# Layer 0's late modulation rows: 32 row products issued inside the attention instead of behind it

## The chip, the core and the metric

The kernel runs on one core of a Trainium2 chip. The metric is the device time of one execution in microseconds (us); less is better. TensorE (PE) multiplies matrices, with its weight loads listed apart (PEld); VectorE (DVE) and ScalarE (ACT) do elementwise work and reductions, GpSimd (POOL) some subtractions, and the queue of SyncE (SP) issues every DMA of this kernel.

## The reference, cut to what matters

Two layers run over 1024 latent tokens and 128 context tokens, 1152 columns in all, of width 1024. Each layer has six modulation vectors for each of the two groups:

```python
def ada_modulation(cond, w_ada, b_ada):
    m = jax.nn.silu(cond) @ w_ada + b_ada
    return jnp.split(m[:, None, :], N_ADA, axis=-1)   # sh1, sc1, g1, sh2, sc2, g2
...
xs = xs + g1_s * ms
xs = xs + g2_s * channel_mixer(modulate(xs, norm_mlp[i], sh2_s, sc2_s), mlp1[i], mlp2[i])
```

Layer 0's `ms` comes from a pooling mixer and an attention of 8 heads. The parts sh2, sc2 and g2 are not needed before layer 0's MLP.

## The kernel before, in words

The activations lie transposed, features on partitions. Precise products are three matmuls of split operands (`mm3`: high by low, low by high, high by high, L335 to L337).

**Modulation rows.** Parts sh1 and sc1 of layer 0 are computed by matmuls. The other parts come from `ada_gen`: 128 modulation values are one tile `f` of 128 weight rows by 1024 (`wada`, 512 KB, two buffers), and for each of the two conditions one DVE instruction multiplies the tile by `silu` (the condition, spread over all partitions) and sums each row (L200, with a read of the accumulator behind it). I call it a row product. When eight tiles are done, `ada_bias` adds the bias (L210, and L214 for the scales). Layer 0's tiles 16 to 31 run as background work in the input projection; the 16 tiles 32 to 47 (sh2, sc2, g2: 32 row products) are the late ones. `bg` is a list of generators, and `background()` takes one step, that is one row product.

**Layer 0's attention.** `max_units` of head h+2 runs beside `attend_units` of head h: 24 score matmuls (`ps_m`, L1034) whose row maxima the DVE takes (L1035); `ps_m` has three PSUM banks, so the fourth matmul waits for the first reduction. The maxima go through `put_max` (L1016, L1020, DMAs to `mrow` and into row 96 of `qh`). `attend_units` has two halves of nine key tiles: three score matmuls (L1070, L1073, L1074), an exponential on ACT, and the value matmul (`ps_pv`, L1077); `finish_values` copies the sum out on the DVE (L1001). For every second head `recip_pair` divides (ACT, POOL L1045, DVE L1046 and L1047).

**Behind the attention.** `x` is loaded again, the pooled and attention outputs are split (`split_groups`, L874 and L875), and `out_group` multiplies them by the output weights, two groups of 384 matmuls (`ps_o`), each tile added to `x` on the DVE (L889). The output weights are split by ACT and, for the low part, POOL (L161). Behind group 0 stand the statistics of the MLP's norm (L271 and L272 on DVE and POOL, then a matmul `ps_n`, L274) and the MLP's operands (L252 to L257, L311, L353). The MLP's first matmul is L422.

The order on each engine is set by a scheduler, by what is ready and by the order of the program, so an instruction may run far from its line. SBUF beyond the constants is 36 slots; the slot longest free is taken next.

Of the kernel before, what the change touches and what calls it, by code (L numbers as in the profile page):

```python
# [35 lines left out]
NEARLY = 2  # L36
# [54 lines left out]
def hybrid_kernel(ctx: ExitStack, tc: tile.TileContext, I, O):  # L91
# [8 lines left out]
    S = Slots(spool, NSLOT)  # L100
# [5 lines left out]
    def PS(name, tag="pa"):  # L106
        return psum.tile([P, 512], F32, tag=tag, name=name, bufs={"pa": 3, "pb": 3, "pc": 2}[tag])
# [4 lines left out]
    def dma(out, in_):  # L112
        nc.sync.dma_start(out.bitcast(F32) if out.dtype == F32R else out,
                          in_.bitcast(F32) if in_.dtype == F32R else in_)

    def run(g):
        for _ in g:
            pass

    def chain(*gs):  # L120
        for g in gs:
            yield from g
# [3 lines left out]
    def after(i, j):  # L126
        tc.add_manual_dep(i.ins, j.ins.name, NOSYNC, reason="order")
        return i
# [24 lines left out]
    def W(tag, name=None):  # L153
        return wpool.tile([P, 1024], F32 if tag == "wr" else F32R, tag=tag, name=name or tag, bufs=3 if tag == "wr" else 4)
# [25 lines left out]
    silu = []  # L180

    def silu_load():
        silu[:] = [S.alloc(f"silu{i}") for i in range(2)]
        for i in range(2):
            dma(silu[i][:, :D].rearrange("p (k f) -> p k f", k=KD), silu_d[:, i, :].partition_broadcast(P))

    def free_silu():
        S.free(*silu)
        yield
# [3 lines left out]
    def ada_gen(layer, fs, ring=False):  # L193
        rs = [] if ring else [S.alloc("wada") for _ in range(2)]
        for f in fs:
            r = W("wr", "wada") if ring else rs[f % 2]
            dma(r[:, :D], I["wada1"][f] if layer else I["wada0t"][f - 16])
            for i in range(2):
                a = ada[layer][:, f, i:i + 1]
                nc.vector.tensor_tensor_reduce(trash, r[:, :D], silu[i][:, :D], scale=1.0, scalar=0.0,  # L200
                                               op0=ALU.mult, op1=ALU.add, accum_out=a)
                yield
            if f % 8 == 7:
                ada_bias(layer, f // 8, ada[layer][:, f - 7:f + 1, :])
        S.free(*rs)

    def ada_bias(layer, part, src):
        a = ada[layer][:, 8 * part:8 * part + 8, :]
        b0 = VEC[f"bada{layer}"][0] + 8 * part
        nc.vector.tensor_add(a, src, vec[:, b0:b0 + 8].unsqueeze(2).to_broadcast([P, 8, 2]))  # L210
        if part in (1, 4):
            n0 = VEC[("nmix" if part == 1 else "nmlp") + str(layer)][0]
            nb = vec[:, n0:n0 + 8].unsqueeze(2).to_broadcast([P, 8, 2])
            nc.vector.scalar_tensor_tensor(a, a, 1.0, nb, op0=ALU.add, op1=ALU.mult)  # L214
# [21 lines left out]
    bg = []  # L236

    def background(n=1):
        for _ in range(n):
            while bg:  # L240
                try:
                    next(bg[0])
                    break
                except StopIteration:
                    bg.pop(0)
# [733 lines left out]
    def load_rest(h):  # L979
        ql, kl, v = S.alloc("ql", F32R), S.alloc("kl", F32R), S.alloc("v")  # L980
        n0, r0 = 64 * (h % 2), 32 * (h % 4)
        dma(ql[0:64, :NS], qd_n[1][h // 2, n0:n0 + 64, :])
        dma(ql[64:96, :NS], qd_r[1][h // 4, r0:r0 + 32, :])
        dma(kl[0:64, :], kd_n[1][h // 2, n0:n0 + 64, :])
        dma(kl[64:96, :], kd_r[1][h // 4, r0:r0 + 32, :])
        load_pv(vd0, h, v)
        return ql, kl, v
# [7 lines left out]
    def load_pv(vd, h, v):  # L995
        o = 192 * (h // 2) + 64 * (h % 2)
        dma(v.rearrange("p (t f) -> p t f", t=9), vd[:, :, o:o + P].rearrange("t p f -> p t f"))

    def finish_values(par, half, po, opair, den, last, store=None):
        qs = slice(half * 512, half * 512 + 512)  # L1000
        nc.vector.tensor_copy(opair[par:par + 64, qs], po[par:par + 64])  # L1001
        nc.scalar.copy(den[par:par + 64, qs], po[64 - par:128 - par])

        def divide():
            recip_pair(opair, den)
            if store is not None:
                dma(store, opair[:, :NS])
                S.free(opair)

        if last:  # L1010
            deferred.append(divide)
# [40 lines left out]
    def later(n=1):  # L1052
        for _ in range(n):
            if deferred:
                deferred.pop(0)()

    def attend_units(h, qk, rest, opair, den):
        (qh, kh), (ql, kl, vv) = qk, rest
        v = vv.rearrange("p (t f) -> p t f", t=9)
        held = None  # L1060
        for half in range(2):
            qs = slice(half * 512, half * 512 + 512)
            po = PS("ps_pv", "pc")
            for kt in range(9):
                if held is None:
                    held, n = S.alloc("p"), 0
                u = slice(512 * n, 512 * n + 512)
                ks = slice(kt * P, kt * P + P)
                ps = PS("ps_st")
                st = nc.tensor.matmul(ps, kl[0:96, ks], qh[0:96, qs], start=True, stop=False)  # L1070
                if len(mxi) >= LAG:
                    after(st, mxi[-LAG])
                nc.tensor.matmul(ps, kh[0:96, ks], ql[0:96, qs], start=False, stop=False)  # L1073
                nc.tensor.matmul(ps, kh[0:97, ks], qh[0:97, qs], start=False, stop=True)  # L1074
                p_ = held[:, u]
                nc.scalar.activation(p_, ps, AF.Exp, scale=scale0)
                nc.tensor.matmul(po, v[:, kt, :], p_, start=kt == 0, stop=kt == 8)  # L1077
                n += 1
                if n == 2:
                    S.free(held)  # L1080
                    held = None
                if kt == 6:
                    later()
                yield
            finish_values(64 * (h % 2), half, po, opair, den, half and h % 2)
        yield
# [4 lines left out]
    weave((chain(max_units(0, qks[0]), max_units(1, qks[1])), 50), (chain(value_gen(), context_gen0()), 17),  # L1091
          (mix_gen(), 13))
    rest = load_rest(0)
    opairs = []
    for h in range(8):
        if h % 2 == 0:
# [13 lines left out]
    S.free(oat)  # L1110


    def ada_late():
        silu_load()
        yield from ada_gen(0, range(16 + 8 * NEARLY, 48))
        S.free(*silu)

    x = [S.alloc(f"x{k}") for k in range(KD)]
    for k in range(KD):
        dma(x[k], I["xT"][k])  # L1120
    acts = [split_groups(o) for o in pooled]
    run(ada_late())
    acts += [split_groups(o) for o in opairs]
    out_group(0, 0, [a[0] for a in acts])
    for a in acts:
# [459 lines left out]
```

## Time and profile before

| | |
|---|---|
| three runs | 3025.92, 3026.92, 3040.58 us; median 3026.92 |
| profiled execution | 3023.98 us, its span 3022.2 us |
| granted TensorE clock, mean | 0.972 of full speed |
| busy | PE 96%, PE weight loads 86%, DVE 71%, ACT 44%, POOL 10% |
| late row products | between 564 and 637 us |
| attention, first score matmul to last value matmul | 312 to 563 us |
| first MLP matmul | 695 us |

The profile is of one execution. A busy PE row is not PE at its peak: consecutive matmuls overlap in the records, so the distance from start to start is what one costs. Idle time in front of an instruction carries the name of what ended it.

### The profile page before, as it was taken

The numbers are of one execution on the slowest core, as the hardware profiler recorded it, in microseconds if no ns is written. First come the engines' busy times: TensorE is split into PE (matmuls) and PEld (weight loads), VectorE is DVE, ScalarE is ACT, GpSimd is POOL, SyncE is SP. The second block draws the span as 40 slices with busy tenths as digits, with TensorE's granted clock in tenths as the row PEclk, the third lists the DMA queues.
The fourth block names the chain that finished last, engine by engine and source line by source line (L and its number), as shares of the span: only waits on it lengthen the run. The fifth ranks groups of instructions, "written<-read, shape, count | busy, mean of one in ns | idle before, by whom it ended". The sixth has DMA issues, their size and how long they took to land.

```text
span 3022.2 us, 46490 instructions
## 1 busy us (share of the span) xinstructions
PE 2910.4 (96%) x18302; PEld 2611.2 (86%) x18302; DVE 2160.5 (71%) x3921; ACT 1330.5 (44%) x2177; POOL 312.7 (10%) x210
## 2 busy tenths in 40 slices
PE   7998999889999999999999999998989999999999
PEld 4956666689999999999988888665889999999999
DVE  5977343797668889777789533677687678777765
ACT  5364344243436543453634522443244355453432
POOL 2004000143000020000221000000030000110000
PEclk9996999999999999999999999998999999999999
DMA  6529331432322334322556537796303232332322
GB/s 234 168 64 318 86 77 44 129 119 77 101 81 92 105 119 154 91 84 84 171 162 214 178 129 194 198 240 165 108 28 99 78 98 84 116 99 78 98 78 87
DMA packets 148268, 372.37 MB, mean 123 GB/s; under 512 B 14225, under 2 KB 67073, under 8 KB 148050
## 3 DMA queue, kind: packets, MB, share of 16 engines
q1 hardware_dynamic: 148050, 369.40, 40.0%
q8 instruction: 144, 2.36, 0.3%
q14 instruction: 74, 0.61, 0.1%
HBM read 310.69 MB, written 57.47 MB: 122 GB/s over the span
## 4 chain that ended last, share of the span: by engine, by line
PE 84%; DVE 6%; DMA 6%; issue 2%; ACT 1%; POOL 1%; SPq 0%; DVEq 0%; POOLq 0%; ACTq 0%
PE ps L452 9%; PE ps L454 9%; PE ps L453 9%; PE ps L422 8%; PE ps L424 8%; PE ps L423 8%; PE ps_pv L1077 4%; PE ps_n L335 2%; PE ps_n L336 2%; PE ps_n L337 2%; DVE trash L200 1%; PE ps_pv L1330 1%; PE ps_v L1354 1%; PE ps_v L1356 1%; PE ps_v L1355 1%
## 5 line engine op out<-in xcount | busy, mean ns | idle before, releaser
L452 PE MATMUL ps<-ml,wh 128*128 128x288 f32 x2048 | 591.9, 295 | 10.3 <-DVE ml L441 7.8
L453 PE MATMUL ps<-mh,wl 128*128 128x288 f32 x2048 | 600.8, 295 | 0.0
L454 PE MATMUL ps<-mh,wh 128*128 128x288 f32 x2048 | 596.6, 295 | 0.0
L422 PE MATMUL ps<-bl,wh 128*128 128x288 f32 x1792 | 532.9, 298 | 13.4 <-DVE bl L353 10.2
L423 PE MATMUL ps<-bh,wl 128*128 128x288 f32 x1792 | 529.7, 296 | 0.0
L424 PE MATMUL ps<-bh,wh 128*128 128x288 f32 x1792 | 528.2, 295 | 0.0
L452 PEld LDWEIGHTS ps<-ml,wh 128*128 128x128 f32 x2048 | 381.2, 188 | 11.3 <-DVE ml L441 8.3
L453 PEld LDWEIGHTS ps<-mh,wl 128*128 128x128 f32 x2048 | 385.1, 188 | 0.0
L454 PEld LDWEIGHTS ps<-mh,wh 128*128 128x128 f32 x2048 | 383.2, 188 | 0.1
L458 DVE SCALAR_TENSOR_TENSOR x<-ps,ada,x 128x288 f32<-128x288 f32 (+2 forms) x640 | 270.1, 451 | 119.1 <-PE ps L454 117.6
L422 PEld LDWEIGHTS ps<-bl,wh 128*128 128x128 f32 x1792 | 336.9, 188 | 16.7 <-issue 11.5
L424 PEld LDWEIGHTS ps<-bh,wh 128*128 128x128 f32 x1792 | 338.4, 189 | 0.0
L423 PEld LDWEIGHTS ps<-bh,wl 128*128 128x128 f32 x1792 | 337.6, 188 | 0.2
L395 ACT CAST wh<-s 128x512 fp32r<-128x512 f32 x256 | 146.1, 618 | 307.0 <-PE ps L454 216.7
L160 ACT CAST wh<-wr 128x1024 fp32r<-128x1024 f32 x188 | 196.9, 1049 | 165.7 <-PE ps L424 79.9
L200 DVE CUSTOM_DVE_ANT_0 trash<-wada,silu 128x1024 bf16<-128x1024 f32 x160 | 217.1, 1357 | 18.2 <-DMA wada<-in_wada 7.6
L161 DVE TENSOR_TENSOR wl<-wr,wh 128x1024 fp32r<-128x1024 f32 x144 | 179.6, 1251 | 44.3 <-ACT wh L160 44.3
L395 ACT CAST wh<-wr 128x1024 fp32r<-128x1024 f32 (+1 forms) x128 | 107.0, 836 | 220.0 <-PE ps L454 155.5
L161 POOL TENSOR_TENSOR wl<-wr,wh 128x1024 fp32r<-128x1024 f32 x44 | 122.2, 2784 | 708.7 <-ACT wh L160 687.4
L1035 DVE TENSOR_REDUCE stat<-ps_m 128x1 f32<-128x384 f32 x192 | 98.3, 552 | 117.0 <-PE ps_m L1034 116.7
L396 DVE TENSOR_TENSOR wl<-s,wh 128x512 fp32r<-128x512 f32 x232 | 157.6, 711 | 5.1 <-ACT wh L395 2.8
L1279 DVE CUSTOM_DVE_ANT_0 trash<-ps_m,ta 128x512 bf16<-128x512 f32 (+1 forms) x128 | 83.5, 652 | 98.1 <-PE ps_m L1277 90.4
(315 smaller groups left out, 6113.8 us busy)
## 6 DMA issues: line engine op xcount, KB each, us to landing
wr<-in_w SPq DMA_DIRECT2D x256, 512.0 KB
wada<-in_wada SPq DMA_DIRECT2D x48, 512.0 KB
wada<-in_wada0t SPq DMA_DIRECT2D x32, 512.0 KB
wr<-in_win SPq DMA_DIRECT2D x24, 512.0 KB
wr<-in_wout SPq DMA_DIRECT2D x24, 512.0 KB
vd<-vst SPq DMA_DIRECT2D x27, 384.0 KB
kk<-kd SPq DMA_DIRECT2D x32, 288.0 KB
nv<-vd SPq DMA_DIRECT2D x16, 576.0 KB
```

Source lines behind the costliest of these rows:

```text
L160: nc.scalar.copy(hi, r)
L161: (nc.gpsimd if e else nc.vector).tensor_sub(lo, r, hi)
L200: nc.vector.tensor_tensor_reduce(trash, r[:, :D], silu[i][:, :D], scale=1.0, scalar=0.0, op0=ALU.mult, op1=ALU.add, accum_out=a)
L395: nc.scalar.copy(h, src)
L396: (nc.gpsimd if j in EDGE and min(ps) in EDGE_POOL else nc.vector).tensor_sub(l, src, h)
L422: nc.tensor.matmul(ps, wh[:, a], hl[:, b], start=k == 0, stop=False)
L423: nc.tensor.matmul(ps, wl[:, a], hh[:, b], start=False, stop=False)
L424: nc.tensor.matmul(ps, wh[:, a], hh[:, b], start=False, stop=k == 3)
L452: nc.tensor.matmul(ps, wh, hl, start=kk == 0, stop=False)
L453: nc.tensor.matmul(ps, wl, hh, start=False, stop=False)
L454: nc.tensor.matmul(ps, wh, hh, start=False, stop=kk == 3)
L458: nc.vector.scalar_tensor_tensor(x[m][:, a:b], ps[:, a - ch * HC:b - ch * HC], g, x[m][:, a:b], op0=ALU.mult, op1=ALU.add)
```

## The change

The 16 late tiles move into the attention. `silu` is loaded, and the generator that makes the products is put on the background list, ahead of the loop over heads; each half head takes two steps of it, at its key tiles 2 and 6, which makes 2 x 2 x 8 = 32. What is left in the list is drained where the late products stood.

```diff
@@ attend_units
                 if kt == 6:
                     later()
+                if kt in (2, 6):
+                    background()
                 yield
@@ ahead of the heads
     rest = load_rest(0)
+    silu_load()
+    bg.append(chain(ada_gen(0, range(16 + 8 * NEARLY, 48)), free_silu()))
@@ behind the heads
-    def ada_late():
-        silu_load()
-        yield from ada_gen(0, range(16 + 8 * NEARLY, 48))
-        S.free(*silu)
-
     acts = [split_groups(o) for o in pooled]
-    run(ada_late())
+    background(10 ** 6)
     acts += [split_groups(o) for o in opairs]
```

The scheduler moves them further. On the DVE, where head 2's maxima begin (just ahead of head 0's first score matmul), there stood before (`ctxw` is the context's softmax, `o` the output of a pair of heads):

```order
L1016 TENSOR_REDUCE stat<-stat 128x8
L1099 COPY o_315_2581<-oat_2166 128x128
L910 TENSOR_REDUCE ctxw_2454<-ps_s 128x4
L911 TENSOR_SCALAR ctxw_2454<-ctxw_2454 128x4
L1035 TENSOR_REDUCE stat<-ps_m 128x1 x7
L916 RECIPROCAL ctxw_2454<-ctxw_2454 128x4
L1035 TENSOR_REDUCE stat<-ps_m 128x1 x2
```

and there stands now:

```order
L910 TENSOR_REDUCE ctxw_2454<-ps_s 128x4
L200 ISA trash,ada_91<-wada_2638,silu_315_2581 128x1024
L200 ISA ada_91 128x1
L1035 TENSOR_REDUCE stat<-ps_m 128x1
L911 TENSOR_SCALAR ctxw_2454<-ctxw_2454 128x4
L1035 TENSOR_REDUCE stat<-ps_m 128x1
L200 ISA trash,ada_91<-wada_2638,silu_316_2582 128x1024
L200 ISA ada_91 128x1
L1035 TENSOR_REDUCE stat<-ps_m 128x1 x3
L916 RECIPROCAL ctxw_2454<-ctxw_2454 128x4
```

The third product stands ahead of head 2's first maximum and the fourth between its second and third; the first two stand just ahead of this piece. From head 0's first score matmul on, the products and maxima ahead of the first L1001 are 13 and 11, ahead of the second 8 and 5, ahead of the third 7 and 9: all 32 are through in the first half of head 1. In the same three half heads of before there are 11, 9 and 9 maxima.

Behind the attention the DVE had, from the last split of the attention's output (`oa`) to the third tile of `x`:

```order
L875 TENSOR_TENSOR oa_4297<-o_495_3910,oa_4297 128x576
L200 ISA trash,ada_91<-wada_4223,silu_573_4219 128x1024
L200 ISA ada_91 128x1
L889 SCALAR_TENSOR_TENSOR x_553_4179<-ps_o,ada_91,x_553_4179 128x288
L200 ISA trash,ada_91<-wada_4223,silu_574_4220 128x1024
L200 ISA ada_91 128x1
L889 SCALAR_TENSOR_TENSOR x_553_4179<-ps_o,ada_91,x_553_4179 128x288
L889 SCALAR_TENSOR_TENSOR x_554_4180<-ps_o,ada_91,x_554_4180 128x288 x2
L200 ISA trash,ada_91<-wada_4224,silu_573_4219 128x1024
```

and has now, from the division of the last pair of heads (L1046) on:

```order
L1046 SCALAR_TENSOR_TENSOR den_3955<-den_3955,ry_4229 128x1024
L1047 SCALAR_TENSOR_TENSOR o_499_3954<-o_499_3954,den_3955 128x1024
L874 CAST oa_4291<-o_438_3495 128x576
L874 CAST oa_4294<-o_499_3954 128x576
L874 CAST oa_4297<-o_499_3954 128x576
L875 TENSOR_TENSOR oa_4291<-o_438_3495,oa_4291 128x576
L875 TENSOR_TENSOR oa_4294<-o_499_3954,oa_4294 128x576
L875 TENSOR_TENSOR oa_4297<-o_499_3954,oa_4297 128x576
L889 SCALAR_TENSOR_TENSOR x_557_4235<-ps_o,ada_91,x_557_4235 128x288 x2
L889 SCALAR_TENSOR_TENSOR x_558_4236<-ps_o,ada_91,x_558_4236 128x288 x2
```

No product is left between them. On PE the order differs only here: the first `ps_n` stands behind 400 output matmuls instead of 411 and the MLP's first matmul behind 368 more instead of 357; from there on PE's order is that of before. 25 output matmuls stand ahead of the last value matmul instead of 28.

In the queue of SP the loads of the attention's start now have products' tiles among them; `kh`, `ql`, `kl` and `v` are head operands, and the last `wada` below waits until its buffer's two products are done:

```order
L113 DMA wada_2637<-in_wada0t 128x1024
L113 DMA vd_486<-vst_2404 128x768
L113 DMA ql_2588<-qdn_479 64x1024
L113 DMA qh_2173<-mrow_2171 1x1024
L113 DMA ql_2588<-qdr_481 32x1024
L113 DMA wada_2638<-in_wada0t 128x1024
L113 DMA wr<-in_wout 128x1024
L113 DMA kl_2589<-kdn_483 64x1152
L113 DMA kl_2589<-kdr_485 32x1152
L113 DMA v_2575<-vd_486 128x9x128
```

Before, `wr`, head 0's row `qh`, head 2's `qh` and `kh` and then `v` stood in this place, and head 2's `kh` stands now ahead of the first `wada`.

## Rows read from the trace of the kernel before

**Rows 1.** The waits of PE between 560 and 700 us: who waited for whom, in us in total, times, and the longest.

```profile
PE ps_o L335 <- DVE oa L875: 10.8, 1, 10.8
PE ps_n L274 <- DVE nt L272: 8.9, 1, 8.9
PE ps_o L335 <- DVE x L889: 4.0, 2, 3.2
```

**Rows 2.** Stretches of the span: from:to, length, then busy us and count of PE, PE's weight loads, DVE, ACT and POOL, the granted clock, the DMA share and GB/s. The first is head 0's two halves and the first half of head 1, the second the other attention, the third from the last value matmul to the first `ps_n`, the fourth from there to the MLP.

```profile
312.28:361.90 49.62, 49.62 (x176) 32.50 (x175) 16.08 (x33) 18.99 (x33) 0.00 (x0) 0.99 0.25 59
361.90:563.40 201.50, 201.50 (x710) 130.22 (x709) 83.61 (x150) 82.46 (x139) 7.12 (x3) 1.00 0.27 73
563.40:637.80 74.40, 54.02 (x386) 52.85 (x385) 70.11 (x98) 16.24 (x26) 26.98 (x13) 0.90 0.46 149
637.80:694.90 57.10, 53.88 (x360) 53.26 (x361) 50.35 (x68) 24.81 (x39) 29.27 (x11) 0.89 0.21 65
```

**Rows 3.** PE in order of time behind the attention: start, us, line, names, and in brackets the idle time ahead with its releaser.

```profile
574.17 0.29 PE L337 MATMUL ps_o<-oa,wh 128*128 128x288 f32 x1
585.22 0.61 PE L335 MATMUL ps_o<-oa,wh 128*128 128x288 f32 x1 [10.75 <-DVE oa L875]
585.62 0.44 PE L336 MATMUL ps_o<-oa,wl 128*128 128x288 f32 x1
585.86 0.44 PE L337 MATMUL ps_o<-oa,wh 128*128 128x288 f32 x1
...
637.78 1.33 PE L274 MATMUL ps_n<-nt,ones 128*128 128x288 f32 x2 [8.88 <-DVE nt L272]
...
686.00 0.61 PE L335 MATMUL ps_o<-oa,wh 128*128 128x288 f32 x1 [3.21 <-DVE x L889]
...
693.73 0.29 PE L337 MATMUL ps_o<-oa,wh 128*128 128x288 f32 x1
...
695.07 0.29 PE L422 MATMUL ps<-bl,wh 128*128 128x288 f32 x1
```

**Rows 4.** DVE and POOL in order of time behind the attention, same columns.

```profile
569.15 3.25 DVE L200 CUSTOM_DVE_ANT_0 trash<-wada,silu 128x1024 bf16<-128x1024 f32 x1 [0.80 <-DMA wada<-in_wada0t]
576.92 1.22 DVE L1046 SCALAR_TENSOR_TENSOR den<-den,ry 128x1024 f32<-128x1024 f32 x1
579.21 1.22 DVE L1047 SCALAR_TENSOR_TENSOR o<-o,den 128x1024 f32<-128x1024 f32 x1
581.86 0.82 DVE L874 CAST oa<-o 128x576 fp32r<-128x576 f32 x2
584.41 1.42 DVE L875 TENSOR_TENSOR oa<-o,oa 128x576 fp32r<-128x576 f32 x2
640.60 1.92 DVE L210 TENSOR_TENSOR ada<-ada,vec 128x16 f32<-128x16 f32 x1
643.24 0.44 DVE L252 TENSOR_SCALAR nt<-ps_n 128x288 f32<-128x288 f32 x1
...
568.92 2.39 POOL L1045 TENSOR_TENSOR den<-den,ry 128x1024 f32<-128x1024 f32 x1 [56.13 <-ACT ry L1044]
571.52 3.13 POOL L161 TENSOR_TENSOR wl<-wr,wh 128x1024 fp32r<-128x1024 f32 x1 [0.20 <-ACT wh L160]
```

**Rows 5.** The row products by line: first the DVE's busy time in those between 563 and 640 us (two records each), then two neighbours of the early products, a stretch of these in which POOL rests, and the DVE's idle time ahead of the products of all 64 products of layer 0.

```profile
563.00:640.00 77.00, 52.67 (x64) 0.89 0.45 146
...
82.74 1.22 DVE L200 CUSTOM_DVE_ANT_0 trash<-wada,silu 128x1024 bf16<-128x1024 f32 x1
84.01 1.23 DVE L200 CUSTOM_DVE_ANT_0 trash<-wada,silu 128x1024 bf16<-128x1024 f32 x1
...
80.00:100.00 20.00, 20.00 (x117) 20.00 (x116) 18.78 (x38) 5.67 (x13) 0.00 (x0) 1.00 0.50 158
...
  DMA wada<-in_wada0t: 7.0, 10
```

**Rows 6.** The attention's first half heads in order of time: score matmuls for the maxima and the value matmul that follows them on PE, three maxima, and the copies that end the first and the third half head.

```profile
318.41 0.69 PE L1034 MATMUL ps_m<-kh,qh 96*128 96x384 f32 x3
318.93 1.02 PE L1077 MATMUL ps_pv<-p,v 128*128 128x512 f32 x2
...
314.43 1.49 DVE L1035 TENSOR_REDUCE stat<-ps_m 128x1 f32<-128x384 f32 x3 [2.25 <-PE ps_m L1034]
...
330.36 0.68 DVE L1001 COPY o<-ps_pv 64x512 f32<-64x512 f32 x1
361.91 0.69 DVE L1001 COPY o<-ps_pv 64x512 f32<-64x512 f32 x1
```

**Rows 7.** Head 2's first maxima, ahead of the attention: the issue of its `kh` on SP, PE's and the DVE's first instruction on it, and the stretch 305 to 310 us with the columns of Rows 2.

```profile
295.53 0.45 SPq L113 DMA_DIRECT2D kh<-kdn  x1
...
303.72 0.76 PE L1034 MATMUL ps_m<-kh,qh 96*128 96x384 f32 x3 [2.48 <-DMA kh<-kdr]
...
304.17 3.34 DVE L1035 TENSOR_REDUCE stat<-ps_m 128x1 f32<-128x384 f32 x7 [2.64 <-PE ps_m L1034]
...
305.00:310.00 5.00, 4.93 (x14) 2.88 (x13) 5.00 (x13) 0.00 (x0) 0.23 (x1) 0.61 1.15 256
```

**Rows 8.** One late tile: its issue on SP and the product that waited for it.

```profile
629.08 0.33 SPq L113 DMA_DIRECT2D wada<-in_wada0t  x1
...
632.83 1.23 DVE L200 CUSTOM_DVE_ANT_0 trash<-wada,silu 128x1024 bf16<-128x1024 f32 x1 [0.15 <-DMA wada<-in_wada0t]
```

## The prediction

> **What bounds the kernel now.** I began with PE's waits by releaser, since PE is the engine that is nearly always busy. Around the moved products three stand out, all of them on the DVE: 10.8, 8.9 and 4.0 us [rows 1]. PE's order of time says where. PE stops after 574.17 + 0.29 us and starts again at 585.22, when the DVE has split the last pair of heads (L875); it stops again ahead of the first `ps_n` at 637.78, for L272, and at 686.00 for an L889. Behind the first stop the output matmuls follow each other by 585.86 - 585.62 = 0.24 us, where undisturbed they need (695.07 - 693.73) / 10 = 0.134 us, the first of those rows and the last being ten matmuls apart [rows 3]. The distance is nearly twice as long: TensorE was at its lower level, 1.2 instead of 2.4 GHz, after standing still for 10.75 us. The stretches say why the DVE is late. From 563.4 to 637.8 it is busy 70.11 of 74.40 us [rows 2], and 52.67 us of this are the late row products [rows 5].
>
> The attention is the opposite. From 312.28 to 361.90 the DVE is busy 16.08 of 49.62 us, from there to 563.40 it is busy 83.61 of 201.50 [rows 2]. PE never rests there.
>
> **What the change gives back behind the attention.** From the last value matmul to the MLP's first matmul the kernel takes 74.40 + 57.10 = 131.5 us [rows 2]. The order leaves 743 output matmuls there; at 0.134 us [rows 3] they need 99.6 us. So 31.9 us are waits, low level and the `ps_n` matmuls. What will remain of them:
> - The division of the last pair still ends it. POOL's L1045 ends at 568.92 + 2.39 = 571.3; behind it the DVE has L1046 and L1047 (1.22 each), three L874 (0.41) and three L875 (0.71) [rows 4], together 5.8 us, to 577.1. PE has work until 574.5 + 3 x 0.134 = 574.9, as three more output matmuls are left behind the last value matmul. A stop of 2.2 us, and up to 2 at the low level behind it; I take 1.
> - The `ps_n` matmuls and their wait. The first `ps_n` has 40 output matmuls between itself and the tile it depends on, 5.4 us, for an addition to `x`, a square, two sums. I take 1 us for the wait (0 to 3) and 2 for the matmuls, two of which are in the row of 1.33 us [rows 3].
> - The stop of 3.21 us for L889 [rows 3]. Today L252 starts at 643.24, 4.1 us after its `ps_n` can be done (637.78 + 1.33), with products' leftovers, L210 of 1.92 us among them, ahead of it [rows 4]. That lateness goes, so I take half, 1.6 us (0 to 3.2).
>
> About 7 us remain (4 to 13): 24.5 us come back (19 to 28).
>
> **What the products cost in the attention.** A product takes 84.01 - 82.74 = 1.27 us from start to start where POOL rests [rows 5]. The late ones take 52.67 / 32 = 1.65 us on average, since one that runs beside POOL's L1045 or L161 takes 3.25 us [rows 4, 5]. The Trainium skill (SBUF — State Buffer, Who interferes with whom) says that a DVE instruction with two SBUF inputs and a GpSimd instruction that reads SBUF exclude each other; the trace agrees here, 3.25 us beside POOL and 1.22 without. By that rule the moved products would take 1.27 us, as POOL rests in these half heads; by today's mean, 28 of them would take 28 x 0.38 = 10.6 us more. I take 1.27 us, since POOL is busy 0.00 us in the first stretch [rows 2].
>
> *Ahead of head 0.* Here the DVE sets the pace: 5.00 of 5.00 us busy from 305 to 310 us [rows 7]. Of the four products there, two lie in idle time (2.64 us, while the load of head 2's `kh` is awaited). The third waits for the second `wada`, which stands behind more loads, and holds up the first maximum; the fourth costs 1.27 us, while two maxima (0.50 each [rows 6]) move behind the start. That makes 0.3 us if the tile is there, and 6 if the third comes some 5 us late. I take 3.
>
> *The first three half heads.* The DVE has to do, from head 0's first score matmul: 28 products, 35.6 us; 25 maxima at 0.50, 12.5; two L210 at 1.92; three L1001 at 0.68 [rows 4 to 6]; 0.5 of small things: 54.4 us. PE needs 49.6 us today, and with four score matmuls fewer (0.52 for three [rows 6]) 48.9. The excess is 5.5 us. It is worst in the first half, 24.6 us of DVE work against 330.36 - 312.28 = 18.1 of PE's, or 6.4 us. It reaches PE because the DVE works in order: a late product holds up the maxima, these the three banks of `ps_m`, and these PE, which has the score matmul in the middle of its own order. If the banks take up the excess, 2 us remain. I take 5.5 (2 to 6.4).
>
> *Late tiles.* Fourteen of the sixteen loads can start only when the two products on their buffer are done, and SP waits there with head 3's loads and the next rows of maxima behind it; these are needed half a head later and more. The DVE waited 7.0 us for tiles of layer 0 over 64 products [rows 5]; half of it, 3.5 us, for 32 (0 to 7). In today's late place nothing hangs on such a wait that the products don't already hold up; in the attention the maxima do.
>
> *POOL* splits two output weights around head 0's start; one may meet a product: 0 to 2.1 us, I take 0. ACT and its exponentials are not touched, and the extra 9 MB of loads lie in stretches with a DMA share of 0.25 to 0.27 [rows 2].
>
> Together 3 + 5.5 + 3.5 = 12 us (2.3 to 21.5).
>
> **Sum.** 24.5 - 12 = 12.5 us less than the profiled 3023.98: 3011.5. The median of the runs is 2.94 us above the profiled execution, which makes 3014.4, say **3014 us**, 0.4% below 3026.92. The ends are 28 - 2.3 = 25.7 us faster and 19 - 21.5, 2.5 us slower.
>
> **The rivals.**
> - *The attention swallows the products.* The DVE has 33.5 us idle in the first stretch and 118 in the second [rows 2]. If the lag runs on behind the banks until the products are through, only the start (about 3 us) is paid: 24.5 - 3 = 21.5 less, **3005 us**. Against it: the order packs 28 products, 35.6 us, into those 33.5.
> - *The tiles land late.* Head 2's `kh` took 303.72 - 295.53 = 8.2 us from its issue to PE's start on it [rows 7]; a late tile took 632.83 - 629.08 = 3.75 [rows 8]. With 8.2 us throughout, two buffers give four products per 2 x 1.27 + 8.2 + 0.3 = 11 us; seven such rounds make 77 us from about 304, so to 381 instead of 361.9. With the start that is 22 us: **3024 us**, no change. For it speaks the crowded queue at the start, against it the share of 0.25 behind that.
> - *Something else binds behind the attention.* Without a product in it the DVE is busy 50.35 of 57.10 us in the fourth stretch, and POOL 29.27 [rows 2]. If only half of the 24.5 us comes back, **3027 us**.
> - *TensorE falls to its lower level in the paced half heads*: the rival on the other side. Where maxima paced PE from 305 to 310 us the granted clock was 0.61 [rows 7]. At the lower level the 48.9 us of PE's work take 0.24 / 0.134 times as long, 38.7 us more: 3014.4 + 38.7 = **3053 us**. It uses up the forecast's 12.5 us once 16 us of PE's work run so. Against it: only one in four or five of PE's matmuls there waits for a maximum, while from 305 to 310 nearly each one did. [...]
>
> **How the numbers follow.** The forecast has 40 in 100, with 3012 to 3021 as its own range; the swallowed products 32, late tiles 14, a second bound behind the attention 6, the lower level 8. The predicted time is that of the forecast. 3003 to 3027 leaves out the lower level and the tails of the others. Half a per cent, 15.1 us, is about what a measurement can tell from no change. Faster by more than that: the swallowed products and the forecast's better end, 0.37; within it 0.55; slower, the lower level, 0.08.
>
> **What would show it.** Right: no product behind 563 us; PE's stop ahead of L875 2 to 3 us long, that of L272 under 3; some 105 to 110 us from the last value matmul to the MLP's first; head 0's first score matmul some 3 us later than at 312.3, and the third L1001 some 12 us later than at 361.9, with PE waiting for L1035. Wrong: third L1001 within 4 us of before (swallowed) or 20 later (late tiles, with waits of the products for `wada`); a granted clock below 0.9 in these half heads; a long stop behind the attention that names POOL or ACT.

## The result, and the profile after

The changed kernel takes 3012.06 us (median of 7 runs, 3006.6 to 3018.45) against 3026.92 (seven runs of before beside it). The ratio is 0.994, with a 95% interval of 0.9926 to 0.9954: 0.5 to 0.7% faster. In two more comparisons it came to 0.9942 and 0.9955. The forecast was 3014. One run of the experiments below (products_in_heads_6_7, 3176.38 us at a granted clock of 0.84) was in a slower state of the chip and stays out of its median, which would be 3009.13 with it.

PE's waits from 280 to 700 us, which answer to [rows 1]: releaser, us in total, times, longest.

```profile
PE ps_m L1034 <- DVE stat L1035: 8.5, 5, 4.4
PE ps_mt L1020 <- DVE stat L1016: 2.7, 1, 2.7
PE ps_o L335 <- DVE oa L875: 2.6, 1, 2.6
PE ps_o L335 <- DVE x L889: 1.3, 1, 1.3
```

The stop ahead of L875 went from 10.8 to 2.6 us, that of L272 is gone, that of L889 went from 4.0 to 1.3. In their place TensorE waits 11.2 us for maxima (L1035) and for `put_max` (L1016), where before waits 1.0 us for maxima and 2.5 for `kh`. Where, the stretches say, with the columns of [rows 2]: from the first product to head 0's first score matmul, from there to the third L1001, from there to the last value matmul, and from there to the MLP.

```profile
303.16:317.87 14.71, 7.96 (x26) 4.83 (x26) 14.42 (x27) 2.53 (x11) 3.17 (x1) 0.62 1.10 261
317.87:373.94 56.07, 53.51 (x175) 33.86 (x174) 46.67 (x88) 19.58 (x34) 0.00 (x0) 0.95 0.69 205
373.94:575.60 201.66, 201.66 (x711) 130.30 (x709) 85.79 (x154) 81.88 (x138) 7.13 (x3) 1.00 0.23 65
575.60:681.30 105.70, 101.83 (x749) 100.92 (x748) 72.13 (x99) 42.00 (x65) 48.73 (x23) 0.98 0.22 65
```

PE in order of time, with the columns of [rows 3]:

```profile
304.54 0.27 PE L1020 MATMUL ps_mt<-ident,stat 128*8 128x128 f32 x1 [2.75 <-DVE stat L1016]
...
310.09 1.22 PE L1034 MATMUL ps_m<-kh,qh 96*128 96x384 f32 x2 [4.45 <-DVE stat L1035]
312.23 2.61 PE L1034 MATMUL ps_m<-kh,qh 96*128 96x384 f32 x5 [0.92 <-DVE stat L1035]
...
317.87 0.80 PE L1070 MATMUL ps_st<-qh,kl 96*128 96x512 f32 x1
...
332.72 0.90 PE L1034 MATMUL ps_m<-kh,qh 96*128 96x384 f32 x2 [1.81 <-DVE stat L1035]
...
589.35 0.40 PE L335 MATMUL ps_o<-oa,wh 128*128 128x288 f32 x1 [2.59 <-DVE oa L875]
...
681.33 0.29 PE L422 MATMUL ps<-bl,wh 128*128 128x288 f32 x1
```

Ahead of head 0 stand 2.75 + 4.45 + 0.92 = 8.1 of the 11.2 us, in the half heads behind it 2.4 (the 1.81 and 0.61 at 373.42). The DVE at these places, in order of time; the last row is the copy that ends the third half head [rows 6]:

```profile
303.16 1.23 DVE L200 CUSTOM_DVE_ANT_0 trash<-wada,silu 128x1024 bf16<-128x1024 f32 x1 [3.96 <-DMA wada<-in_wada0t]
304.31 0.17 DVE L1016 TENSOR_REDUCE stat<-stat 128x8 f32<-128x24 f32 x1
304.40 2.28 DVE L1103 COPY o<-oat 128x128 f32<-128x128 f32 x1
306.60 1.21 DVE L200 CUSTOM_DVE_ANT_0 trash<-wada,silu 128x1024 bf16<-128x1024 f32 x1
308.35 1.21 DVE L200 CUSTOM_DVE_ANT_0 trash<-wada,silu 128x1024 bf16<-128x1024 f32 x1
...
329.69 1.23 DVE L200 CUSTOM_DVE_ANT_0 trash<-wada,silu 128x1024 bf16<-128x1024 f32 x1 [2.55 <-DMA wada<-in_wada0t]
...
370.05 1.23 DVE L200 CUSTOM_DVE_ANT_0 trash<-wada,silu 128x1024 bf16<-128x1024 f32 x1 [3.23 <-DMA wada<-in_wada0t]
373.94 0.69 DVE L1001 COPY o<-ps_pv 64x512 f32<-64x512 f32 x1
```

The first product waits 3.96 us for its tile with `put_max` (L1016) behind it, and PE's transpose waits for that. SP's issues show why tiles were late: the first stands behind three heads' operands, and its product starts 8.1 us after its issue; the third is issued only behind three issues of `v`, which take 7.42 us.

```profile
295.03 0.36 SPq L113 DMA_DIRECT2D wada<-in_wada0t  x1
...
303.98 7.42 SPq L113 DMA_DIRECT2D v<-vd  x3
...
314.14 0.37 SPq L113 DMA_DIRECT2D wada<-in_wada0t  x1
```

So the changed kernel's MLP begins at 681.3 instead of 695.1, 13.7 us earlier, yet its profiled execution (3018.45) is only 5.5 us below that of before. The difference lies in layer 1's attention, first and last score matmul for its maxima, before and after:

```profile
1758.90:2105.80 346.90, 329.94 (x1720) 246.62 (x1719) 187.79 (x491) 128.58 (x281) 18.29 (x30) 0.94 0.74 197
```

```profile
1744.80:2099.70 354.90, 335.10 (x1721) 250.39 (x1720) 188.44 (x491) 129.26 (x280) 18.07 (x29) 0.92 0.73 194
```

PE's order there is the same. Behind the MLP's first matmul the profiled executions of this study took from 2327 us (the one of before) to 2348. Medians of a few runs can differ by some us through this alone, so I price the experiments by places in the trace ahead of it.

### The profile page after: what moved, and what is told of

Its sections match the earlier page's. It is cut to its first block, busy times and chain, and to the rows that moved or that the text cites. A ratio compares the mean times of both kernels' runs of the same rounds, so it can differ in the third digit from the quotient of the medians.

```text
span 3016.6 us, 46513 instructions
## 1 busy us (share of the span) xinstructions
PE 2914.8 (97%) x18302; PEld 2612.8 (87%) x18302; DVE 2149.4 (71%) x3921; ACT 1331.9 (44%) x2177; POOL 306.9 (10%) x210
## 4 chain that ended last, share of the span: by engine, by line
PE 80%; DVE 6%; DMA 6%; issue 5%; ACT 2%; POOL 1%; SPq 0%; DVEq 0%; POOLq 0%; ACTq 0%
PE ps L452 9%; PE ps L454 9%; PE ps L453 9%; PE ps L422 8%; PE ps L424 8%; PE ps L423 8%; PE ps_n L335 2%; PE ps_n L336 2%; PE ps_n L337 2%; PE ps_pv L1329 2%; PE ps_o L335 1%; PE ps_o L336 1%; PE ps_o L337 1%; PE ps_pv L1077 1%; PE ps_v L1353 1%
## 5 line engine op out<-in xcount | busy, mean ns | idle before, releaser
L452 PEld LDWEIGHTS ps<-ml,wh 128*128 128x128 f32 x2048 | 381.5, 188 | 11.3 <-DVE ml L441 8.3
L200 DVE CUSTOM_DVE_ANT_0 trash<-wada,silu 128x1024 bf16<-128x1024 f32 x160 | 203.2, 1270 | 28.0 <-DMA wada<-in_wada0t 16.4
L161 DVE TENSOR_TENSOR wl<-wr,wh 128x1024 fp32r<-128x1024 f32 x144 | 179.6, 1251 | 46.6 <-ACT wh L160 46.5
L161 POOL TENSOR_TENSOR wl<-wr,wh 128x1024 fp32r<-128x1024 f32 x44 | 119.3, 2718 | 701.9 <-ACT wh L160 686.2
L1035 DVE TENSOR_REDUCE stat<-ps_m 128x1 f32<-128x384 f32 x192 | 99.3, 551 | 77.8 <-PE ps_m L1034 77.4
```

What stands on the lines that cost most here:

```text
L161: (nc.gpsimd if e else nc.vector).tensor_sub(lo, r, hi)
L452: nc.tensor.matmul(ps, wh, hl, start=kk == 0, stop=False)
```

## The experiments

The table holds all runs: head 0's first score matmul, the third L1001 and the MLP's first matmul in each profile (us), and the time with its ratio to before on the same chip. A time is the median of the kernel's runs, a place comes from one profile. The places themselves differ by 2 to 4 us between executions of one program (the three changed rows), so a difference of 2 us between two rows says nothing.

| kernel | score | third L1001 | MLP | median | ratio, interval |
|---|---|---|---|---|---|
| before | 312.3 | 361.9 | 695.1 | 3026.92 | 1 |
| changed | 317.9 | 373.9 | 681.3 | 3012.06 | 0.9940, 0.9926 to 0.9954 |
| changed_again | 315.8 | 370.6 | 679.7 | 3010.82 | 0.9942, 0.9923 to 0.9962 |
| changed_third | 315.7 | 371.7 | 677.6 | 3015.22 | 0.9955, 0.9937 to 0.9973 |
| no_late_products | 310.8 | 362.9 | 668.4 | 3006.77 | 0.9910, 0.9886 to 0.9935 |
| loads_without_products | 315.0 | 373.2 | 678.8 | 3020.97 | 0.9959, 0.9941 to 0.9977 |
| loads_read_by_gpsimd | 311.4 | 367.2 | 674.3 | 3009.83 | 0.9939, 0.9915 to 0.9963 |
| two_resident_tiles | 315.4 | 365.9 | 674.5 | 3010.44 | 0.9943, 0.9921 to 0.9965 |
| four_tile_buffers | 320.7 | 373.4 | 683.7 | 3013.26 | 0.9942, 0.9920 to 0.9963 |
| products_from_head_1 | 313.4 | 369.4 | 678.4 | 3012.45 | 0.9947, 0.9927 to 0.9968 |
| from_head_1_four_buffers | 313.6 | 363.3 | 673.2 | 3006.44 | 0.9923, 0.9904 to 0.9942 |
| products_from_head_2 | 313.0 | 364.5 | 675.3 | 3015.86 | 0.9945, 0.9923 to 0.9966 |
| products_in_heads_6_7 | 311.2 | 362.6 | 669.8 | 3007.59 | 0.9921, 0.9895 to 0.9947 |
| heads_6_7_again | 312.9 | 364.5 | 671.7 | 3013.79 | 0.9942, 0.9920 to 0.9963 |

**The floor.** In `ada_gen`, for layer 0's tiles from 32 on:

```diff
-            dma(r[:, :D], ...)
-            for i in range(2):
+            if late: nc.vector.tensor_copy(ada[0][:, f, :], ada[0][:, f - 16, :])
+            else: dma(r[:, :D], ...)
+            for i in range(0 if late else 2):
```

> The 16 late tiles are neither loaded nor multiplied; sh2, sc2 and g2 take copies of other rows instead, so this kernel leaves 32 row products out. It gives the floor of the change. Theory of the sum: the traces put the products' price in the attention at 5.6 us ahead of head 0 (first score matmul at 317.87 instead of 312.28) and 6.4 us in the next three half heads, 12.0 us together, and nothing behind that, so 3012.06 - 12.0 = 3000 us; first score matmul near 312.3, last value matmul near 563.6, the MLP's first matmul some 105.7 us behind that. Rival 'the layer 1 stretch belongs to the change': the trace of the changed kernel also has 8.0 us more in layer 1's attention than the trace before; if the moved products cause these (through other buffers or a shifted queue), this kernel gets them back too and comes to 2992.

Its MLP begins at 668.4, 26.7 us earlier than that of before: so much did the products cost in their late place. The changed kernel gets 13.7, 15.4 and 17.5 us of it (its three profiles), and pays 13.0, 11.3 and 9.2: 10.5, 8.7 and 8.2 of that up to the last value matmul, the rest behind it, where the floor's 103.3 us are the least of all. The median agrees: 3006.77 lies 25.4 us below that of before on its chip (3032.2). Behind the MLP's first matmul this profile took 2331 us, and the three of the changed kernel 2335, 2328 and 2335, so the rival's 8 us don't go with the products. The two stretches of this kernel that serve as a measure below, from the first score matmul to the third L1001 and the one behind the attention:

```profile
310.80:362.94 52.14, 52.14 (x175) 34.20 (x174) 15.62 (x32) 18.99 (x33) 0.00 (x0) 0.94 0.37 89
...
565.10:668.37 103.27, 99.58 (x743) 98.66 (x742) 69.22 (x94) 41.88 (x65) 48.79 (x23) 1.00 0.21 67
```

**The loads alone.** The product becomes a copy of one column:

```diff
+                if layer == 0 and f >= 32:
+                    nc.vector.tensor_copy(a, r[:, i:i + 1])
+                    yield; continue
                 nc.vector.tensor_tensor_reduce(trash, ...)
```

> The 16 late tiles are loaded in the same place, but a copy of one column stands for each row product (the 32 products' sums are left out), so the queue and the buffers have nearly the same work and the DVE has none. Theory of the sum, DVE work is the price: the 6.4 us of the three half heads go and of the 5.6 at the start at most 2 remain: 3000 to 3002. Rival 'late tiles and a crowded queue are the price': 3006 to 3010, with the first score matmul again near 317 us.

The theory of my sum fell here. With nearly no DVE work left the price is that of the changed kernel: third L1001 at 373.2, MLP at 678.8, and a ratio (0.9959) whose interval overlaps those of the changed kernel. Its time, 3020.97, lies above both ranges that I had given. The stretch from the first score matmul to the third L1001:

```profile
315.02:373.18 58.16, 54.38 (x175) 34.86 (x174) 17.92 (x62) 18.89 (x33) 0.00 (x0) 0.92 0.70 201
```

The DVE is busy 17.92 of 58.16 us, and TensorE still takes 6.0 us more than without late tiles. What the DVE does instead, its waits from 295 to 375 us:

```profile
DVE ada L201 <- DMA wada<-in_wada0t: 33.8, 14, 5.8
DVE stat L1039 <- PE ps_m L1038: 12.2, 5, 3.7
```

It stands 33.8 us in front of tiles, with maxima behind it.

**The work alone.** `dma` only for `f < 34`, so that all products read the first two tiles:

```diff
+            if layer or f < 34:
-            dma(r[:, :D], ...)
+                dma(r[:, :D], ...)
```

> All 32 products run in the attention, but only the first two late tiles are loaded and all products read these two, so 14 loads are left out (sh2, sc2 and g2 are partly wrong rows). Theory 'late tiles' (the copies of a column in place of the products cost as much as the products: third L1001 at 373.2 against 362.9 without either): without the loads most of the price goes, third L1001 at 363 to 367, the MLP's first matmul at 670 to 673. Theory of the sum, 'the DVE's work paces the maxima': the excess of 5.5 us and 1 to 3 at the start stay, third L1001 at 369 to 372, the MLP's first matmul at 676 to 679. If both are prices that cover each other, this kernel lies like the loads alone, above 372.

Third L1001 at 365.9, in the range of the late tiles. The price lies ahead of head 0 (315.4, the floor's 310.8); at most 2.5 us of it are the DVE's waits for the two tiles that are still loaded. Two of TensorE's stops there, 0.92 and 0.98 us, stand behind one product each, so at the start, where the DVE sets the pace, its work does reach TensorE. Behind the start there is no price; the three half heads, and the first of them:

```profile
315.40:365.85 50.45, 50.45 (x172) 33.15 (x171) 45.13 (x86) 18.99 (x33) 0.00 (x0) 0.96 0.29 76
...
315.40:336.88 21.48, 21.48 (x72) 14.66 (x71) 21.24 (x40) 7.54 (x13) 0.00 (x0) 0.90 0.28 73
```

The DVE is busy 21.24 of 21.48 us and TensorE never stops: 50.45 us for the three, where before needs 49.62 and the floor 52.14. The excess of DVE work that I put at 5.5 us costs TensorE nothing that can be measured. L1001 is a copy on the DVE and can come late by itself, so here is the whole attention by TensorE alone, from the first score matmul to the last value matmul: before 251.4 us, the floor 254.3, the changed kernel 257.7, 258.0 and 257.6, the loads alone 259.5, the work alone 253.3. That says the same. The MLP at 674.5 is 1.5 us later than I had given for the late tiles.

**Who waits: the DVE or the queue.** `nc.gpsimd.tensor_copy` in place of `nc.vector.tensor_copy` in the loads alone.

> As the loads without products, but GpSimd copies the column of each late tile instead of the DVE (the 32 products' sums are left out again). The 16 loads, their buffers and their place in the queue stay; only the wait for a tile no longer stands among the maxima. Theory 'the DVE waits in order for tiles and holds up the maxima': the price of 9.5 us (last value matmul at 574.1 against 564.7 without late tiles) goes to 0 to 3 us: last value matmul at 565 to 568, the MLP's first at 669 to 672, and no wait of TensorE for a maximum of more than 1 us. Rival 'the loads delay other loads' (kh, v and the rows of maxima behind them in the queue): the price stays at 7 us or more, with TensorE waiting for kh, v or qh, last value matmul at 571 to 575.

The same loads, and third L1001 at 367.2 instead of 373.2, MLP at 674.3 instead of 678.8: 10.2 us of price become 4.2, and 10.4 become 5.9. That lies between the two ranges that I had given. At the third L1001 the longer part is the DVE's wait in order. The rest does not go to the rival by this run, since the DVE still waited in order, now for the bias (L214) that reads the copies:

```profile
DVE stat L1039 <- PE ps_m L1038: 27.2, 10, 3.8
DVE ada L214 <- POOL ada L201: 17.1, 2, 9.2
```

But a part of it is the queue: TensorE stops here for `kh`, which it does in no other kernel behind head 0's start but the one with four buffers, and once longer for a maximum than the 1 us that I had allowed:

```profile
PE ps_m L1038 <- DMA kh<-kdn: 1.6, 1, 1.6
PE ps_m L1038 <- DVE stat L1039: 1.4, 1, 1.4
```

**More buffers, another start, both.** First four buffers for the late tiles (`rs[f % len(rs)]`):

```diff
-        rs = ... for _ in range(2)]
+        rs = ... for _ in range(4 if fs[0] == 32 else 2)]
```

> The changed kernel with four buffers for the late tiles instead of two, nothing left out. Theory 'two buffers make the tiles late' (a load can start only when two products are done): the waits of 2.6 and 3.2 us in the half heads go, third L1001 at 367 to 371. Theory 'the crowded queue at the start makes them late': the loads stand behind and ahead of the same loads of v, qh and kl, two more of them crowd the start, and third L1001 stays at 372 to 376, the first score matmul at 317 to 320. Theory 'DVE work': no change, 373 to 375.

Neither theory alone was right: each was right in its own place. From the first score matmul on the price is gone (52.70 us, the floor's 52.14), with the DVE as busy as in the changed kernel; but the start moved to 320.7, with one stop of 6.26 us. In front of the maximum that ends it, the DVE waits 3.99 us for the first tile, and the tile's second product takes 3.23 us beside POOL's split; the later stops of 0.99 us stand behind one product each. So not the queue alone makes the start dear.

```profile
320.71:373.41 52.70, 51.76 (x171) 33.58 (x170) 45.74 (x87) 18.99 (x33) 0.00 (x0) 0.94 0.61 172
```

```profile
309.70 1.62 PE L1034 MATMUL ps_m<-kh,qh 96*128 96x384 f32 x3 [6.26 <-DVE stat L1035]
```

Then the generator is put on the list at head 1, with two buffers:

```diff
-    silu_load(); bg.append(...)            # ahead of the heads
     for h in range(8):
+        if h == 1: silu_load(); bg.append(...)
```

> All 32 products are kept, put on the list at head 1 instead of ahead of head 0, two steps at key tiles 2 and 6. It takes the products from the start, where the queue loads three heads' operands, and leaves nearly the same density (4, 9, 9, 9 and 1 in the first five half heads). Theory 'the crowded start is the price': first score matmul at 311 to 313, third L1001 at 363 to 366, the MLP's first matmul at 669 to 673. Theory of the sum: start gone but pacing stays, third L1001 at 367 to 370. Theory 'two buffers': also 367 or later, with the DVE waiting over 8 us for tiles in the half heads.

The start is cheap (313.4), but the third L1001 is at 369.4, in the range of the sum and of the two buffers, and the fourth 8.3 us behind the floor's (386.2 against 377.9). As a price both are too high: TensorE does not stop between its first score matmul and the third L1001, and does 187 matmuls there instead of 175, so the copy itself was late on the DVE. The last value matmul is 7.5 us behind the floor's. The DVE waits 6.3 us for tiles here (8 had been given), and PE's rows show how such a wait arrives, with the low level behind it (a pair of value matmuls takes 1.80 us instead of 1.02; the granted clock from 388.5 to 391.5 is 0.52):

```profile
384.68 1.02 PE L1077 MATMUL ps_pv<-p,v 128*128 128x512 f32 x2
385.13 0.74 PE L1034 MATMUL ps_m<-kh,qh 96*128 96x384 f32 x1
387.54 0.44 PE L1034 MATMUL ps_m<-kh,qh 96*128 96x384 f32 x1 [1.67 <-DVE stat L1035]
...
388.52 1.80 PE L1077 MATMUL ps_pv<-p,v 128*128 128x512 f32 x2
```

Last, head 1 and four buffers together:

> All 32 products, put on the list at head 1 as before, with four buffers for the late tiles. With four buffers the changed kernel took 52.7 us from the first score matmul to the third L1001, as without late tiles (52.1), but started at 320.7; from head 1 the start was at 313.4, but the DVE waited 6.3 us for tiles. Theory 'tiles are late for want of buffers, except at the start, where the queue is crowded': both remedies together leave the DVE's work alone, last value matmul at 566 to 569 (two resident tiles: 568.3), the MLP's first at 672 to 675. Rival 'the DVE's work beside the maxima is the price at this density': as from head 1 with two buffers, last value matmul at 571 to 573, the MLP's first at 677 to 679.

The DVE's waits for tiles shrink, and the attention has no price left: 64.61 us from the first score matmul to the fourth L1001, 67.07 without any late products (at granted clocks of 1.00 and 0.95) and 64.6 in before, with 53.62 us of DVE work in them. Its waits for tiles, its stretch, and the same stretch of the floor:

```profile
DVE trash L200 <- DMA wada<-in_wada0t: 1.8, 2, 0.9
```

```profile
313.62:378.23 64.61, 64.61 (x224) 41.59 (x223) 53.62 (x101) 24.94 (x43) 0.00 (x0) 1.00 0.64 189
```

```profile
310.80:377.87 67.07, 67.07 (x225) 43.56 (x224) 19.56 (x41) 25.07 (x44) 0.00 (x0) 0.95 0.34 82
```

The last value matmul starts at 563.15, earlier than I had expected. With four buffers the stop ahead of L875 is 4.4 us in both kernels, and the part behind the attention takes 109 instead of 106 us. The order differs there: the DVE has four casts (L874) and four L875 behind the last division instead of three each, and TensorE has 682 output matmuls behind the stop instead of 667, 15 more of 0.134 us. Why the order is so, no run here tells.

**Where no maxima are.** Generator at head 2 with four steps, or at head 6 with eight steps in each half head:

```diff
-                if kt in (2, 6):
+                if kt in (1, 3, 5, 7):      # at head 2; range(1, 9) at head 6
                     background()
```

> All 32 products are kept, put on the list at head 2 with four steps in each half head: six half heads have 6 to 9 of them beside 9 to 14 maxima. Theory of the sum: the start's 5.6 us go; a half head of 9 products and 10 maxima is 9 x 1.27 + 10 x 0.50 = 16.4 us of DVE work against 15.8 of TensorE's, so pacing costs at most 1 to 2 us: 3001 to 3003. Rival 'late tiles': the loads are as late as in the changed kernel, where the DVE waited some 9 us for tiles inside the attention, and 4 to 6 us remain: 3004 to 3007.

The MLP begins at 675.3, 7.0 us behind the floor: nearer to the 4 to 6 of the late tiles (the DVE waits 8.3 us for them) than to the 1 to 3 of the sum.

> All 32 products are kept, but the generator is put on the list at head 6 with eight steps in each half head, where no maxima are left for the DVE. Theory 'maxima and start are the price': products ahead of head 0's start and between maxima cost the 12.0 us, so without either the time is that of the kernel without late products, 3000 us (2998 to 3003), first score matmul near 312.3, no stop of TensorE in heads 5 to 7. Rival 'late tiles': 16 loads through two buffers and the one queue delay head 7's and the output weights' loads wherever they stand; then 3004 to 3008, with TensorE waiting in heads 6 and 7 or at the start of the output group. Rival 'the end of the attention': the products push the last division or the splits of the pooled outputs back, and TensorE's stop ahead of L875 grows from 2.6 to 5 us or more.

> The products in heads 6 and 7 again, beside the changed kernel on one chip. By the places of the two traces (the MLP's first matmul at 669.8 against 681.3 and 679.7) it should be 10 to 11.5 us faster than the changed kernel, by the two medians against before (23.1 and 17.2 us) some 6; 4 to 12 us.

> The changed kernel, as the partner of the run ahead of it: 3008 to 3013 us where before has its median of 3027, the MLP's first matmul at 679 to 682.

The scheduler moved 11 of the 32 products forward into head 5, nine of them beside eleven maxima in one half head, and TensorE still never stops; here are the last three heads:

```profile
473.90:564.10 90.20, 90.20 (x317) 57.23 (x315) 69.73 (x122) 36.04 (x62) 2.79 (x1) 1.00 0.49 164
```

The MLP begins at 669.8 and 671.7, 1.5 and 3.3 us behind the floor. Beside the changed kernel on one chip that is 5.9 us earlier, but the medians differ by 1.4 us only, less than I had expected, and the intervals overlap. Of the two better placements, only the one from head 1 with four buffers lies apart from the changed kernel on one chip (3006.44 against 3015.22), with intervals that overlap a little; it is the best version that the runs point to. **changed_again** is the changed kernel itself once more:

> The changed kernel itself, on the chip of the three kernels beside it. Its places should come again within 1 us if they are set by the program (first score matmul 317.9, third L1001 373.9, last value matmul 575.1, the MLP's first matmul 681.3); what lies behind the MLP's first matmul has so far taken between 2327 and 2341 us in six kernels whose order is the same there, so the median may differ by some us from 3012.06.

It came 2 us earlier at the start and 1.6 at the MLP, so the places are not exact to 1 us as I had expected.

## Why the prediction was right, and which of its terms were not

**The number** held: 3012.06 for 3014, at the lower edge of the forecast's own range of 3012 to 3021. The medians lie 14.9 us apart, just short of the half per cent (15.1 us); the ratio over all runs, 0.6%, lies just past it, on the side to which I had given 0.37, and its interval (0.46 to 0.74%) reaches a little to the other side.

**The back end** was right in its steps. 24.5 us were to come back (the remainders that the prediction lists make 7.8 us, so 24.1 by its own items); the 131.5 us of [rows 2] became 105.7, which is 25.8 back, and 25.5 and 27.1 in the two other profiles. The stop ahead of L875 was to be 2.2 us and is 2.6, but not as I had it: L1045 ends 6.6 us behind the start of the last value matmul, where I took 7.6, and the three L874 take 3.36 us instead of 1.23, since one of them lasts 2.62 us beside POOL's L161 (2.63 us in the two other profiles). Without that the stop would be some 0.5 us, an estimate from these rows:

```profile
584.59 3.36 DVE L874 CAST oa<-o 128x576 fp32r<-128x576 f32 x3
...
585.14 2.50 POOL L161 TENSOR_TENSOR wl<-wr,wh 128x1024 fp32r<-128x1024 f32 x1 [2.99 <-ACT wh L160]
```

Behind the stop the low level cost 1.5 us (14 matmuls at 0.24 instead of 0.134), where 1 was taken. The wait for L272, for which I kept 1 us, is gone; L889's is 1.3, where 1.6 was taken. 105.7 us from the last value matmul to the MLP lie in the 105 to 110, the third profile's 104.3 just below.

**Ahead of head 0** I took 3 us of 0.3 to 6; it was 5.6, 3.5 and 3.4. I had the second tile late; it was the first, and what it held up was `put_max` and the transpose behind it. Behind that, a product between the first maxima stops TensorE again, for 0.92 us. How the start's price divides between tiles, work and POOL, no run separates: the loads alone start at 315.0, the work with its two tiles at 315.4.

**The three half heads** are where the reasoning failed. The sum had 5.5 us for the DVE's excess of work and 3.5 for late tiles, 9 in all; the three profiles have 6.4, 5.2 and 6.4. The step that failed is "it reaches PE because the DVE works in order: a late product holds up the maxima". The order holds, but what reached PE was the wait in it, not the work: with the work and no loads the half heads take 0.8 us more than before, with the loads and no work 8.5 more (against the floor, whose first half head also runs in part at the low level, 1.7 less and 6.0 more). The sum itself was also too large: it had 54.4 us of DVE work, and the trace has 46.67, less than the 48.9 of PE. Its 28 products make 34.2 us instead of 35.6, its two L210 0.3 instead of 3.8, and neighbouring records overlap. And it compared totals, while in order of time a saturated DVE (21.24 of 21.48 us) still gave each maximum before PE needed it. I named that possibility ("if the banks take up the excess") and chose the other end. The term for late tiles was too small for the opposite reason: it was half of the 7.0 us that the 64 products waited in their old places [rows 5], where the queue is not shared with the heads' operands. So a term of 5.5 that should have been about 0, one of 3.5 that should have been about 6, and a start of 3 that was 3.4 to 5.6 gave 12 where the profiles have 12.0, 8.7 and 9.8. That sum was right by cancellation. TensorE's recorded stops make 2.4, 3.4 and 3.0 us of the 6.4, 5.2 and 6.4; the low level explains some of the rest in the first profile (granted clock 0.95), and what is left stays open.

**POOL** was taken at nothing. In the first profile it did not meet a product, and all 32 run undisturbed (min, median, max in ns):

```profile
L200 DVE CUSTOM_DVE_ANT_0 trash<-wada,silu x32: 1204/1222/1227, 303.2 to 371.7; 128x1024 bf16<-128x1024 f32 x32
```

That is the term of 1.27 us with its read, and not the late ones' mean of 1.65. But POOL's split at the start met a copy instead (below), which took 2.28 us, and 2.31 in the second profile; in the third it met a product, which took 1.95. So the 0 for POOL was too low, inside the 0 to 2.1 that I had given, and it is part of the start's price.

**The rivals.** "The attention swallows the products" (3005) is right as to the DVE's work and wrong as to the tiles; from head 1 with four buffers it is what happens (3006.4). "The tiles land late" (3024) named the cause of nearly all of the price inside, and had it three times too large: 8.2 us for each tile would have put the third L1001 at 381, and it stood at 371 to 374. No stop behind the attention names POOL or ACT, though by the rows above POOL makes 2.1 us of the stop for L875, through the DVE. The lower level came for some us only: the granted clock of the three half heads is 0.95 (before 0.99), and 0.94 without any late product, where only the first half head is low. In the first half head of the changed kernel's first profile it was 0.89, just below the 0.9 that I had named as a sign of this rival, and in its second profile 1.00.

## What to carry to other kernels

When work moves to an engine with idle time, sum not only its busy time but ask what it waits for. Here the DVE's waits for tiles, 33.8 us in 14 waits with the loads alone, held up the maxima behind them and cost TensorE 6 us, while products of 1.2 us between maxima cost nothing that could be measured once the half heads had begun. At the start, where the DVE already set the pace, a product stopped TensorE for 0.9 to 1.0 us. So place moved work where its loads do not share the queue with the start of a stage, and give it buffers for the landing time (8 us at the start, 2.5 us of products for each tile: more than two). A total that comes out right is no proof of its terms; the run that keeps the loads and drops the work, and its opposite, tell them apart.

## What the runs showed of the hardware

A DVE copy of 128x128 (L1103) took 2.28 us ahead of head 0, from 304.40 to 306.68, where its like in the kernel before (L1099) took 0.23 at 299.22, ahead of POOL's split. POOL's row in the changed kernel:

```profile
303.42 3.17 POOL L161 TENSOR_TENSOR wl<-wr,wh 128x1024 fp32r<-128x1024 f32 x1 [13.89 <-ACT wh L160]
```

It ends at 306.59, and the copy with it. L210 of before, 1.92 us to 642.52 [rows 4], likewise ends with a pair of POOL's splits; in the attention, where POOL rests, it takes 0.17. The copy and the splits of before, then L210 of the changed kernel:

```profile
299.22 0.23 DVE L1099 COPY o<-oat 128x128 f32<-128x128 f32 x1 [0.46 <-ACT oat L954]
...
637.37 5.12 POOL L161 TENSOR_TENSOR wl<-wr,wh 128x1024 fp32r<-128x1024 f32 x2
```

```profile
342.95 0.17 DVE L210 TENSOR_TENSOR ada<-ada,vec 128x16 f32<-128x16 f32 x1
```

I had read the 1.92 us as the price of the instruction; by these rows nearly all of it was a wait for POOL. The Trainium skill (SBUF — State Buffer, Who interferes with whom) counts copies that can enter a two-port mode among what excludes GpSimd, beside the instructions with two SBUF inputs; the trace agrees in both places, 2.28 against 0.23 and 1.92 against 0.17.
